# Pre-norm factors from moments gathered in the sub-layer before, and a reworked state-space stage, in a six-sub-layer decode kernel

## The chip, the cores and the metric

The kernel runs on one core of a Trainium2 chip. The number that counts is the device time of one execution in microseconds (us). The core has five engines that run beside each other, each in its own program order: TensorE (PE) multiplies matrices, VectorE (DVE), ScalarE (ACT) and GpSimd (POOL) work on elements, SyncE (SP) issues transfers. They wait for each other by semaphores.

## The reference

576 tokens (512 of a prompt, 64 of eight samples) go through six sub-layers. Each has the same frame: a root-mean-square norm ahead (pre-norm), the sub-layer, a norm behind (post-norm), and the sum with the residual.

```
def rms_norm(x, g):
    y = x * lax.rsqrt(jnp.mean(x * x, axis=-1, keepdims=True) + 1e-6)
    return y * g
# sub-layers 0, 2, 3, 5: SwiGLU, 1024 -> 2816 -> 1024
h = (silu(n @ w_gate) * (n @ w_up)) @ w_down;      x = x + 0.5 * rms_norm(h, post)
# sub-layer 1: state-space layer (S5) and a gated linear unit (GLU)
s_t = a * s_(t-1) + g * (B u_t);  y = Re(C s_t) + d * u_t          # per group of 16 channels
z = gelu(y) @ w_glu;  h = z[:1024] * sigmoid(z[1024:]);            x = x + rms_norm(h, post)
# sub-layer 4: latent attention (prompt: causal; samples: paged cache), then @ w_o
```

The data are float32. Everything that a token needs of a norm is one number: the reciprocal root of its mean square over 1024 channels.

## The kernel before

Channels lie on the partitions in eight blocks of 128, tokens along the free axis in two halves of 288. `X` is the residual, `Y` the output of the sub-layer, `XH` and `XL` (one tile, `XHL`) a high and a low part of the input of the next one. A large product is three matmuls of 288 columns (`mm3`, L156 to L158): high by high, high by low, low by high. `unit` makes 48 such matmuls (gate and up of 128 channels, one half), a down block (`down`) 33, a block of the attention's output 24. Weights come as `raw` from SP, ACT writes their high part `whi`, DVE the low part `wlo` (L151).

A norm is worked out by `stats`: the squares of all blocks are added into `ACC` (ACT squares, POOL adds, L147), a matmul with one column per 72 tokens sums over the partitions (L103; in the last block of the sub-layer its square comes as a tile of its own, `sqd`), nine small DVE operations on 72x4 elements take the reciprocal root (L107 to L116; called the chain below), a tenth writes it as a diagonal tile `rs_d` (L119), and `spread` (L127) is the matmul that lays it on all partitions, in PSUM for the post-norm, in `R` for the pre-norm.

Between two sub-layers the order is written out by hand in `tail` and `first_units` (called a boundary below). For each half: post statistics, spread, then `post` (L209 multiplies `Y` by gain and factor, L211 adds to `X`, `xsplit` writes `XH` and `XL`), then `squares` of the new `X` for the next pre-norm. Half 1's post statistics and its `post` are put off: `first_units` issues them after input blocks 0 and 2 of the next sub-layer's first four products of half 0. The gain-only input is used in the products; the pre-norm factor is multiplied in behind them, in `evac`. So a boundary has four spreads, in this order: post half 0, post half 1, pre half 0, pre half 1. There is such a boundary into sub-layers 2, 3, 4 and 5; the one into the S5 layer (sub-layer 1) is in `s5_mixer`; the last sub-layer has only its own post-norm.

The S5 layer runs as a pipeline over eight blocks k of 128 channels: `s_u` (normalized input `un`, loads), `s_a` (transpose into `TT`), `s_b` (transpose into `U`), `s_c` (product with table WV, rotation), `s_s` (scan), `s_d` (products with tables `CKb` and `mk`), `s_e` (transpose back, direct term d*u, gelu, split). Its tables are made during sub-layer 0 from a list of small pieces (`s5_pieces`); `tick`, called after each evacuation there, issues the next few, so that they lie beside the matmuls. Table parts go through DRAM: RT, CA, KT, WV; the last piece writes the table MD from KT in eight transfers (L618).

## Time and profile before

| | |
|---|---|
| time, median of 3 runs | 2487.06 us (2482.69 to 2488.77) |
| the profiled execution | 2486.95 us, its span 2485.2 us |
| TensorE busy | 2381.8 us, 96% |
| VectorE / ScalarE / GpSimd busy | 1281.5 / 873.6 / 556.1 us |
| mean granted clock of TensorE | 0.978 |

A profile is one execution. A line names the engine, the line of the kernel, the operation, the tiles (out, then in), and how many. "[1.86 <-DVE rs_d L119]" behind an instruction says that its engine sat idle 1.86 us before it, and what ended that. The granted clock is the share of full speed that TensorE got in a stretch. A matmul is pipelined: its own duration overlaps with the next, and the step from start to start is what it costs.

### The profile page before, as it was taken

What the parts mean: (1) busy time and instruction counts of PE and PEld (TensorE: products, weight loads), DVE (VectorE), ACT (ScalarE), POOL (GpSimd) and SP (SyncE); (2) the same over time, 40 slices, a digit from 0 to 9 for tenths busy, and PEclk for the clock granted to TensorE, in tenths of its full rate; (3) what the DMA queues carried; (4) which work ended last, traced back from release to release, by engine and by line L of the source; (5) the groups of instructions that cost most, each with busy time, mean ns of one, the idle gap of its engine ahead of it and who ended that gap; (6) DMA issues with size and microseconds to landing.
All of it is one profiled execution on the core that took longest, in us unless ns stands there. A gap on an engine that the chain in (4) does not pass through costs nothing.

```text
span 2485.2 us, 44160 instructions
## 1 busy us (share of the span) xinstructions
PE 2381.8 (96%) x17610; PEld 2313.1 (93%) x17610; DVE 1281.5 (52%) x2647; ACT 873.6 (35%) x1807; POOL 556.1 (22%) x819
## 2 busy tenths in 40 slices
PE   7999999789989999998999999899999999999998
PEld 7999999679989999998999999798888898999997
DVE  7564565685464233347432433767777655423434
ACT  4222322353332222224222222434666653222221
POOL 3123535452231001124100112530000042100112
PEclk9999999799989999998999999999999999999999
DMA  3224343473212222222223222345555332222221
GB/s 126 86 86 146 126 130 118 125 188 97 77 60 86 71 92 86 75 88 68 80 67 101 86 70 76 114 114 178 169 173 179 130 104 69 75 74 99 86 71 63
DMA packets 114642, 254.89 MB, mean 103 GB/s; under 512 B 25122, under 2 KB 53539, under 8 KB 114179
## 3 DMA queue, kind: packets, MB, share of 16 engines
q1 hardware_dynamic: 114434, 252.06, 32.0%
q8 instruction: 139, 2.28, 0.4%
q14 instruction: 69, 0.56, 0.1%
HBM read 231.79 MB, written 22.59 MB: 102 GB/s over the span
## 4 chain that ended last, share of the span: by engine, by line
PE 68%; DVE 6%; ACT 2%; issue 1%; POOL 1%; DMA 1%; SPq 0%; ACTq 0%; DVEq 0%; POOLq 0%
PE ps L158 20%; PE ps L156 20%; PE ps L157 20%; PE ps L1331 2%; PE ps L1296 2%; DVE XHL L153 1%; DVE t L209 1%; POOL X L211 1%; PE ps L127 1%; PE ps L1237 1%; DVE wlo L151 1%; PE ps L1317 0%; PE ps L757 0%; PE ps L1225 0%; ACT Pm L1198 0%
## 5 line engine op out<-in xcount | busy, mean ns | idle before, releaser
L156 PE MATMUL ps<-XHL,whi 128*128 128x288 f32 x3344 | 1002.4, 300 | 20.4 <-ACT whi L151 12.9
L157 PE MATMUL ps<-XHL,whi 128*128 128x288 f32 x3344 | 998.7, 299 | 4.7 <-DVE XHL L153 4.7
L158 PE MATMUL ps<-XHL,wlo 128*128 128x288 f32 x3344 | 995.9, 298 | 1.4 <-DVE wlo L151 1.4
L156 PEld LDWEIGHTS ps<-XHL,whi 128*128 128x128 f32 x3344 | 638.2, 191 | 24.3 <-ACT whi L151 13.5
L157 PEld LDWEIGHTS ps<-XHL,whi 128*128 128x128 f32 x3344 | 639.0, 191 | 9.6 <-DVE XHL L153 7.4
L158 PEld LDWEIGHTS ps<-XHL,wlo 128*128 128x128 f32 x3344 | 637.9, 191 | 2.2 <-DVE wlo L151 2.0
L151 DVE TENSOR_TENSOR wlo<-raw,whi 128x1024 fp32r<-128x1024 f32 (+2 forms) x349 | 409.3, 1198 | 317.3 <-ACT whi L151 316.6
L151 ACT ACTIVATE whi<-raw 128x1024 fp32r<-128x1024 f32 (+2 forms) x349 | 321.6, 946 | 446.0 <-PE ps L157 378.2
L158 PE MATMUL ps<-HH,wlo 128*128 128x288 f32 x1408 | 415.8, 296 | 1.9 <-DVE wlo L151 1.9
L156 PE MATMUL ps<-HH,whi 128*128 128x288 f32 x1408 | 417.3, 296 | 0.0
L157 PE MATMUL ps<-HL,whi 128*128 128x288 f32 x1408 | 415.3, 295 | 0.0
L316 POOL TENSOR_TENSOR t<-t,t 128x288 f32<-128x288 f32 x176 | 143.1, 813 | 1113.2 <-DVE t L315 983.5
L158 PEld LDWEIGHTS ps<-HH,wlo 128*128 128x128 f32 x1408 | 265.2, 188 | 2.6 <-DVE wlo L151 2.6
L156 PEld LDWEIGHTS ps<-HH,whi 128*128 128x128 f32 x1408 | 265.3, 188 | 0.4
L157 PEld LDWEIGHTS ps<-HL,whi 128*128 128x128 f32 x1408 | 265.3, 188 | 0.2
L315 DVE TENSOR_TENSOR t<-ps,R 128x288 f32<-128x288 f32 x176 | 80.2, 456 | 331.3 <-PE ps L158 331.1
L147 POOL TENSOR_TENSOR ACC<-ACC,sq 128x288 f32<-128x288 f32 x137 | 138.3, 1010 | 391.2 <-ACT sq L143 387.0
L314 ACT ACTIVATE t<-t 128x288 f32<-128x288 f32 x176 | 77.9, 444 | 329.6 <-DVE t L313 313.2
L151 ACT ACTIVATE HH<-t 128x288 fp32r<-128x288 f32 x176 | 77.2, 439 | 249.0 <-POOL t L316 242.2
L151 DVE TENSOR_TENSOR HL<-t,HH 128x288 fp32r<-128x288 f32 x176 | 81.7, 465 | 125.2 <-ACT HH L151 124.8
L313 DVE TENSOR_TENSOR t<-ps,R 128x288 f32<-128x288 f32 x176 | 79.3, 450 | 53.8 <-PE ps L158 47.9
L369 DVE TENSOR_TENSOR Y<-ps,Y 128x288 f32<-128x288 f32 x64 | 29.2, 455 | 129.4 <-PE ps L158 129.4
(332 smaller groups left out, 2612.9 us busy)
## 6 DMA issues: line engine op xcount, KB each, us to landing
raw<-GU SPq DMA_DIRECT2D x176, 512.0 KB, 4.1
pgr<-PG SPq DMA_DIRECT2D x128, 320.0 KB, 3.5
raw<-DN SPq DMA_DIRECT2D x64, 512.0 KB, 3.5
raw<-DN SPq DMA_DIRECT2D x64, 192.0 KB, 3.4
raw<-GLU SPq DMA_DIRECT2D x16, 512.0 KB, 4.2
CAd<-s5w SPq DMA_DIRECT2D x8, 576.0 KB, 3.6
WVd<-s5w SPq DMA_DIRECT2D x8, 512.0 KB, 3.4
wv<-WVd SPq DMA_DIRECT2D x8, 512.0 KB, 5.8
```

Source lines behind the costliest of these rows:

```text
L147: (add or G).tensor_tensor(acc, acc, sq, op=OP.add)
L151: return A.activation(hi, src, AF.Copy), V.tensor_tensor(lo, src, hi.bitcast(F32), op=OP.subtract)
L156: P.matmul(o, wh, xh, start=st, stop=False)
L157: P.matmul(o, wh, xl, start=False, stop=False)
L158: P.matmul(o, wl, xh, start=False, stop=sp)
L313: V.tensor_tensor(t, pp[0], R[:, hs(h)], op=OP.mult)
L314: A.activation(s, t, AF.Silu)
L315: V.tensor_tensor(u, pp[1], R[:, hs(h)], op=OP.mult)
L316: g = G.tensor_tensor(u, u, s, op=OP.mult)
L369: ins = V.tensor_tensor(y, o, y, op=OP.add)
L1296: P.matmul(so, qb[:, cb], d["kv"][u][:, :, 256 + cb * 128:384 + cb * 128], start=cb == 0, stop=False)
L1331: P.matmul(o, d["pt"][:, c], d["kv"][i // 2][:, i % 2, 0:256], start=i == 0, stop=i == 3)
```

## The change

Five things change.

1. The sum of squares of the new residual is no longer taken from the new residual. With y the post factor of a token, x' = x + y*g*Y, so the sum of x'^2 is SA + 2*y*sum(x*g*Y) + y^2*sum((g*Y)^2). `SA` (72x2x4) carries the sum of x^2 from stage to stage. During the last pass of a sub-layer `ymom` gathers, beside the sum of Y^2 in `ACC`, the other two in `R` and `ACQ`: one more ACT square, one DVE product, two more adds per block and half (POOL; the third add on DVE in the attention). `mom_a` makes the post factor and the gathered sums of a half, `mom_b` the pre factor. `squares` and the statistics ahead of a first unit go.
2. In the S5 layer half 1's `post` is done block by block inside the pipeline (`post1`), `un` is written by ACT with the gain alone, and the pre factor is multiplied in when `TT` is written, in eight ACT copies per block (two before).
3. The direct term d*u is put in the table (KO gets M16*d), so the addition in `s_e` goes; POOL's operations in the S5 loop (L730, L739, L779) go to DVE or into other operations.
4. The transfers of the table pieces (RT, CA, KT, WV and the loads of B and C) are issued some pieces behind the work that makes their data; the list has 201 pieces instead of 177 and is spread over 46 ticks instead of 52 behind the first 20.
5. `evac` of the feed-forward layers applies Silu in place.

```
+        def mom_a(h, SQ, nxt):
+
+            src = sums([[ACC[:, hs(h)], SQ[h][0]]])
+            q = cur["sm"].tile([CP, 4], F32, name="rs_a")
+            V.tensor_scalar(q, src, 1e-6, None, op0=OP.add)
+            y = rsqrt(q)
+            d = diag(y)
+            bc = None
+            if nxt is not None:
+                pbc = sums([[R[:, hs(h)], SQ[h][1]], [ACQ[:, hs(h)], SQ[h][2]]])
+                bc = cur["sm"].tile([CP, 8], F32, name="rs_bc")
+                V.tensor_copy(bc, pbc)
+            return y, d, bc
...
+        def mom_b(h, y, d_, bc):
+
+            m = cur["sm"].tile([CP, 4], F32, name="rs_m")
+            V.tensor_tensor(m, bc[:, 4:8], y, op=OP.mult)
+            V.scalar_tensor_tensor(m, bc[:, 0:4], 2.0, m, op0=OP.mult, op1=OP.add)
+            V.tensor_tensor(m, m, y, op=OP.mult)
+            V.tensor_tensor(SA[:, h], SA[:, h], m, op=OP.add)
+            V.tensor_scalar(SA[:, h], SA[:, h], 0.0, None, op0=OP.max)
+            q = cur["sm"].tile([CP, 4], F32, name="rs_ab")
+            V.tensor_scalar(q, SA[:, h], 1e-6, None, op0=OP.add)
+            return rsqrt(q, "b")
...
+        def ymom(n, m, h, y, nxt, sc=1.0):
+
+            g = GP[:, n, 1, m:m + 1]
+            out = []
+            for i, acc in enumerate((ACC, R, ACQ)):
+                dst = acc[:, hs(h)] if m == 0 else (smt("t1") if i else sqd.tile([128, H], F32, name="sqd")) if m == 7 else smt("sq")
+                if i == 1:
+                    V.scalar_tensor_tensor(dst, y, g, X[:, m, hs(h)], op0=OP.mult, op1=OP.mult)
+                else:
+                    A.activation(dst, y, AF.Square, scale=g if i else sc)
+                if 0 < m < 7:
+                    (V if n == 4 and i == 2 else G).tensor_tensor(acc[:, hs(h)], acc[:, hs(h)], dst, op=OP.add)
+                out.append(dst)
+                if nxt is None:
+                    break
+            return out
...
-            d0 = stats([ACC[:, hs(0)], SQ[0]])
+            z = [mom_a(0, SQ, nxt)]
             blk(mlast[0], 1)
...
-            squares(0, nxt, last)
-            d1 = []
-            state["pend"] = [lambda: d1.append(stats([ACC[:, hs(1)], SQ[1]])), lambda: post(n, 1, spread(d1[0]), nxt)]
+            state["mom"] = z
+            if nxt == 1:
+                s5["D0"] = mom_b(0, *z[0])
...
+                def half1():
+                    z.append(mom_a(1, SQ, nxt))
+                    spread(z[1][1], ACC[:, hs(1)])
+                    s5["D1"] = mom_b(1, *z[1])
+                    end = state["chain"].ins
+
+                    def blk1(k):
+                        with tc.issue_after(end) if k else nullcontext():
+                            post1(n, 1, ACC[:, hs(1)], nxt, k)
+                    s5["post"] = blk1
+                state["pend"] = [half1]
+                return
+            state["pend"] = [lambda: z.append(mom_a(1, SQ, nxt)), lambda: post(n, 1, spread(z[1][1]), nxt)]
...
-            d0 = stats([ACC[:, hs(0)]])
+            z = state["mom"]
+            d0 = diag(mom_b(0, *z[0]))
...
-                        d1 = stats([ACC[:, hs(1)]])
+                        d1 = diag(mom_b(1, *z[1]))
...
                 def diag():
-                    S.dma_start(s5["CA"][k], CA.rearrange("p g r d i -> p g r (d i)"))
+                    S.dma_start(s5["RT"][k], RT)
...
-                    S.dma_start(s5["KT"][k], KO)
+
+                    V.scalar_tensor_tensor(KO[:, 0:16], M16, dn[:, k:k + 1], pk[:, 0:16], op0=OP.mult, op1=OP.add)
...
+                def store():
+                    S.dma_start(s5["KT"][k], S_["KO"])
                     S.dma_start(s5["WV"][k], WT.rearrange("p g r d i -> p g r (d i)"))
-                out = [load] + [rot(i) for i in range(6)] + last
-                last[:] = [prods]
-                out += [lambda hf=hf, j=j, st=st: table(*(((CA, PW, 9, 1, hf, True), (WT, PG, 8, 0, hf, False))[st]))[j]()
+                out = [load] + [rot(i) for i in range(6)]
+                out[2:2] = last[:1]
+                out[5:5] = [bc]
+                out += last[1:2]
+                tabs = [lambda hf=hf, j=j, st=st: table(*(((CA, PW, 9, 1, hf, True), (WT, PG, 8, 0, hf, False))[st]))[j]()
                         for st in range(2) for hf in range(2) for j in range(2)]
-                return out + [diag]
+                tabs[2:2] = last[2:]
+                last[:] = [store_ca, prods, store]
+                return out + tabs + [diag]
...
-                u = UN[k] = lp.tile([128, T], F32, name="un", bufs=4)
-                if k:
-                    V.scalar_tensor_tensor(u, X[:, k], GP[:, n, 0, k:k + 1], R, op0=OP.mult, op1=OP.mult)
...
+                if k:
+                    scaled(k)
+
+            def scaled(k):
+                s5["post"](k)
+                u = UN[k] = lp.tile([128, T], F32, name="un")
+                for h in range(2):
+                    A.activation(u[:, hs(h)], X[:, k, hs(h)], AF.Copy, scale=GP[:, n, 0, k:k + 1])
...
+                u = UN.pop(k)
                 for h in range(2):
                     pt = psum()
                     for j in range(4):
-                        P.transpose(pt[:CP, (3 - j) * 128:(4 - j) * 128], UN[k][:, (4 * h + j) * CP:(4 * h + j + 1) * CP], ident)
-                    A.activation(TT[:, :, 4 - 4 * h:8 - 4 * h].rearrange("p g j i -> p j g i"),
-                                 pt[:CP].rearrange("p (j g i) -> p j g i", j=4, g=8), AF.Copy)
+                        P.transpose(pt[:CP, j * 128:j * 128 + 128], u[:, (4 * h + j) * CP:(4 * h + j + 1) * CP], ident)
+                    for j in range(4):
+                        A.activation(TT[:, :, 7 - 4 * h - j], pt[:CP, j * 128:j * 128 + 128].rearrange("p (g i) -> p g i", g=8),
+                                     AF.Copy, scale=DD[h][:, j:j + 1])
...
-                    G.tensor_tensor(m1[:, :, gq], m1[:, :, gq], m2[:, :, gq], op=OP.add)
+                    V.tensor_tensor(m1[:, :, gq], m1[:, :, gq], m2[:, :, gq], op=OP.add)
...
-                G.tensor_tensor(m1, Z, RT[:, 0:1].to_broadcast([128, 2, 4, 64]), op=OP.mult)
+                V.tensor_tensor(m1, Z, RT[:, 0:1].to_broadcast([128, 2, 4, 64]), op=OP.mult)
...
                         P.transpose(pt[:, j * CP:j * CP + CP], YT[:, 4 * h + j], ident[:CP, :CP])
-                    y, w, sq = smt("t2"), smt("t3"), smt("sq")
-                    V.scalar_tensor_tensor(y, u[:, hs(h)], s5["dn"][:, k:k + 1], pt[:, :H], op0=OP.mult, op1=OP.add)
-                    A.activation(sq, y, AF.Square)
-                    yy.append((y, w, sq))
+                    w, sq = smt("t3"), smt("sq")
+                    A.activation(sq, pt, AF.Square)
+                    yy.append((pt, w, sq))
                 for y, w, sq in yy:
-                    V.tensor_scalar(w, sq, 0.044715, 1.0, op0=OP.mult, op1=OP.add)
-                    G.tensor_tensor(w, w, y, op=OP.mult)
-                    A.activation(w, w, AF.Tanh, scale=float(np.sqrt(2 / np.pi)))
+                    V.scalar_tensor_tensor(w, sq, 1 / 0.044715, y, op0=OP.add, op1=OP.mult)
+                    A.activation(w, w, AF.Tanh, scale=float(np.sqrt(2 / np.pi) * 0.044715))
                 for h, (y, w, sq) in enumerate(yy):
-                    V.scalar_tensor_tensor(y, w, 1.0, y, op0=OP.add, op1=OP.mult)
-                    split(XH[:, k, hs(h)], XL[:, k, hs(h)], y, 0.5)
+                    V.scalar_tensor_tensor(sq, w, 1.0, y, op0=OP.add, op1=OP.mult)
+                    split(XH[:, k, hs(h)], XL[:, k, hs(h)], sq, 0.5)
...
-            end = min(len(pcs), max(done[0], 20 + (len(pcs) - 20) * (done[0] - 20) // 52))
+            end = min(len(pcs), max(done[0], 20 + (len(pcs) - 20) * (done[0] - 20) // 46))
```

The order on three engines, before and after.

On TensorE, from the S5 boundary's half-1 statistics to the first product of the S5 loop (L723 before, L785 after; `un` is the input, `TT` its transpose). Before:

```order
L127 MATMUL ps<-rs_d,ones 128x288
L103 MATMUL ps<-ones,ACC 72x1 x4
L103 MATMUL ps<-ones,sq_5476 72x1 x4
L692 MATMUL ps<-ident,un 72x128 x4
L103 MATMUL ps<-ones,sq_5478 72x1 x4
L103 MATMUL ps<-ones,sq_5480 72x1 x4
L103 MATMUL ps<-ones,sq_5482 72x1 x4
L692 MATMUL ps<-ident,un 72x128 x4
L103 MATMUL ps<-ones,sq_5484 72x1 x4
L711 MATMUL ps<-ident,TT 128x72 x8
L127 MATMUL ps<-rs_d,ones 128x288 x2
L723 MATMUL ps<-U_5559,wv 64x72 x16
```

After:

```order
L106 MATMUL ps<-ones,ACC 72x1 x4
L106 MATMUL ps<-ones,R 72x1 x4
L106 MATMUL ps<-ones,ACQ 72x1 x4
L106 MATMUL ps<-ones,sqd 72x1 x4
L106 MATMUL ps<-ones,t_5428 72x1 x4
L106 MATMUL ps<-ones,t_5430 72x1 x4
L187 MATMUL ps<-rs_d,ones 128x288
L761 MATMUL ps<-ident,un 72x128 x8
L773 MATMUL ps<-ident,TT 128x72 x8
L785 MATMUL ps<-U_5569,wv 64x72 x16
```

The six sums of the new residual's squares and two spreads between the post spread and the loop are gone; four sums stand ahead of the post spread instead.

On VectorE, at the boundary into sub-layer 3, around the diagonal tile of the pre factor of half 0. Before, from the last input splits of half 1 (`XHL`) to the first evacuation (L313):

```order
L153 SCALAR_TENSOR_TENSOR XHL<-X,GP,XHL 128x288 x4
L107 TENSOR_SCALAR rs_a<-ps 72x4
L108 TENSOR_SCALAR rs_y<-rs_a 72x4
L110 SCALAR_TENSOR_TENSOR rs_t<-rs_y 72x4
L111 TENSOR_TENSOR rs_t<-rs_t,rs_a 72x4
L112 SCALAR_TENSOR_TENSOR rs_y<-rs_t,rs_y 72x4
L113 SCALAR_TENSOR_TENSOR rs_t<-rs_y 72x4
L114 TENSOR_TENSOR rs_t<-rs_t,rs_a 72x4
L115 SCALAR_TENSOR_TENSOR rs_t<-rs_t 72x4
L116 SCALAR_TENSOR_TENSOR rs_y<-rs_t,rs_y 72x4
L119 SCALAR_TENSOR_TENSOR rs_d<-ident,rs_y 72x288
L313 TENSOR_TENSOR t_12245<-ps,R 128x288
```

After (names in `a` belong to the post factor of half 1, those in `b` to the pre factor of half 0):

```order
L121 SCALAR_TENSOR_TENSOR rs_ya<-rs_ta,rs_ya 72x4
L127 SCALAR_TENSOR_TENSOR rs_d<-ident,rs_ya 72x288
L127 SCALAR_TENSOR_TENSOR rs_d<-ident,rs_yb 72x288
L158 TENSOR_TENSOR rs_m<-rs_bc,rs_ya 72x4
L159 SCALAR_TENSOR_TENSOR rs_m<-rs_bc,rs_m 72x4
L160 TENSOR_TENSOR rs_m<-rs_m,rs_ya 72x4
L265 SCALAR_TENSOR_TENSOR t_12237<-Y,GP,ps 128x288
L265 SCALAR_TENSOR_TENSOR t_12242<-Y,GP,ps 128x288
L267 TENSOR_TENSOR X<-X,t_12237 128x288
```

The chain of the pre factor of half 0 stood behind all of half 1's post work; now its diagonal tile is written ahead of that work, beside the one of the post factor of half 1.

On GpSimd, the same boundary: adds of squares into `ACC`, adds of the post-norm into `X`, and the first gate products (L316 before, L371 after). Before:

```order
L147 TENSOR_TENSOR ACC<-ACC,sq 128x288 x7
L211 TENSOR_TENSOR X<-X,t_12081 128x288
L211 TENSOR_TENSOR X<-X,t_12086 128x288
L211 TENSOR_TENSOR X<-X,t_12091 128x288
L211 TENSOR_TENSOR X<-X,t_12101 128x288
L211 TENSOR_TENSOR X<-X,t_12106 128x288
L211 TENSOR_TENSOR X<-X,t_12111 128x288
L147 TENSOR_TENSOR ACC<-ACC,sq 128x288 x7
L316 TENSOR_TENSOR t_12247<-t_12247,t_12246 128x288
```

After:

```order
L178 TENSOR_TENSOR R<-R,sq 128x288
L178 TENSOR_TENSOR ACQ<-ACQ,sq 128x288
L267 TENSOR_TENSOR X<-X,t_12061 128x288
L267 TENSOR_TENSOR X<-X,t_12066 128x288
L267 TENSOR_TENSOR X<-X,t_12071 128x288
L267 TENSOR_TENSOR X<-X,t_12081 128x288
L267 TENSOR_TENSOR X<-X,t_12086 128x288
L267 TENSOR_TENSOR X<-X,t_12091 128x288
L267 TENSOR_TENSOR X<-X,t_12242 128x288
```

Both runs of seven adds between and behind the residual adds are gone; adds into `R` and `ACQ` stand ahead of them, in the last pass.

## Rows read from the trace of the kernel before

**Rows 1.** The page: TensorE's busy time, share of the span, instructions.

```profile
PE 2381.8 (96%) x17610; PEld 2313.1 (93%) x17610; DVE 1281.5 (52%) x2647; ACT 873.6 (35%) x1807; POOL 556.1 (22%) x819
```

**Rows 2.** TensorE's waits over the span: us in total, times, longest us.

```profile
PE ps L127 <- DVE rs_d L119: 35.2, 13, 4.8
PE ps L723 <- ACT U L712: 5.8, 5, 1.7
```

**Rows 3.** Stretches: length, TensorE busy (matmuls), granted clock, DMA share, GB/s.

```profile
1080.00:1120.00 40.00, 39.05 (x294) 1.00 0.28 90
1120.00:1160.00 40.00, 32.10 (x208) 0.83 0.16 53
```

**Rows 4.** Timeline of TensorE, boundary into sub-layer 3: start, us, instruction, idle before.

```profile
1109.89 0.65 PE L127 MATMUL ps<-rs_d,ones 72*128 72x288 f32 x2
...
1130.26 1.14 PE L127 MATMUL ps<-rs_d,ones 72*128 72x288 f32 x2 [1.86 <-DVE rs_d L119]
...
1139.28 0.40 PE L156 MATMUL ps<-XHL,whi 128*128 128x288 f32 x1 [1.65 <-ACT XHL L153]
...
1146.87 1.30 PE L127 MATMUL ps<-rs_d,ones 72*128 72x288 f32 x2 [3.70 <-DVE rs_d L119]
...
1159.38 0.65 PE L127 MATMUL ps<-rs_d,ones 72*128 72x288 f32 x2
```

**Rows 5.** Timeline of VectorE there: first and last step of two chains.

```profile
1106.69 0.16 DVE L107 TENSOR_SCALAR rs_a<-ps 72x4 f32<-72x4 f32 x1 [1.62 <-PE ps L103]
...
1108.43 0.45 DVE L119 SCALAR_TENSOR_TENSOR rs_d<-ident,rs_y 72x288 f32<-72x288 f32 x1
...
1125.62 0.14 DVE L107 TENSOR_SCALAR rs_a<-ps 72x4 f32<-72x4 f32 x1
...
1129.26 0.94 DVE L119 SCALAR_TENSOR_TENSOR rs_d<-ident,rs_y 72x288 f32<-72x288 f32 x1
```

**Rows 6.** Timeline of GpSimd there.

```profile
1124.71 7.01 POOL L147 TENSOR_TENSOR ACC<-ACC,sq 128x288 f32<-128x288 f32 x7 [2.82 <-ACT sq L143]
```

**Rows 7.** Timeline of TensorE there: a one-column sum and what follows it.

```profile
1135.33 0.62 PE L103 MATMUL ps<-ones,ACC 128*72 128x1 f32 x8
1135.81 0.38 PE L156 MATMUL ps<-XHL,whi 128*128 128x288 f32 x1
```

**Rows 8.** Timeline of TensorE, start of the S5 loop and its third and fourth step.

```profile
466.17 1.30 PE L127 MATMUL ps<-rs_d,ones 72*128 72x288 f32 x2 [4.75 <-DVE rs_d L119]
...
480.77 1.22 PE L711 MATMUL ps<-ident,TT 72*128 72x72 f32 x8 [4.14 <-ACT TT L694]
481.79 2.22 PE L127 MATMUL ps<-rs_d,ones 72*128 72x288 f32 x4
483.94 1.35 PE L723 MATMUL ps<-U,wv 128*64 128x72 f32 x18
...
503.00 1.22 PE L723 MATMUL ps<-U,wv 128*64 128x72 f32 x32
...
513.03 0.28 PE L723 MATMUL ps<-U,wv 128*64 128x72 f32 x2 [0.80 <-ACT U L712]
```

**Rows 9.** Groups of four S5 steps (503 to 543 us): busy us, mean ns, idle before.

```profile
L778 DVE TENSOR_SCALAR t<-sq 128x288 f32<-128x288 f32 x8 | 6.7, 834 | 0.2 <-ACT sq L775 0.2
L669 DVE SCALAR_TENSOR_TENSOR un<-X,GP,R 128x576 f32<-128x576 f32 x4 | 5.1, 1285 | 0.0
L740 DVE TENSOR_TENSOR Y<-Y,rt 128x512 f32<-128x512 f32 x4 | 5.1, 1277 | 0.0
L701 ACT ACTIVATE TT<-ps 72x512 f32<-72x512 f32 x8 | 4.7, 589 | 1.8 <-PE ps L700 1.8
```

**Rows 10.** The page's groups over the span: busy us, mean ns of one.

```profile
L147 POOL TENSOR_TENSOR ACC<-ACC,sq 128x288 f32<-128x288 f32 x137 | 138.3, 1010 | 391.2 <-ACT sq L143 387.0
L314 ACT ACTIVATE t<-t 128x288 f32<-128x288 f32 x176 | 77.9, 444 | 329.6 <-DVE t L313 313.2
L315 DVE TENSOR_TENSOR t<-ps,R 128x288 f32<-128x288 f32 x176 | 80.2, 456 | 331.3 <-PE ps L158 331.1
```

**Rows 11.** Timeline of VectorE, then GpSimd, in sub-layer 2's last pass.

```profile
1070.58 2.31 DVE L151 TENSOR_TENSOR wlo<-raw,whi 128x1024 fp32r<-128x1024 f32 x2 [0.55 <-ACT whi L151]
...
1071.02 1.46 POOL L147 TENSOR_TENSOR ACC<-ACC,sq 128x288 f32<-128x288 f32 x1 [3.91 <-ACT sq L143]
1075.11 0.80 POOL L147 TENSOR_TENSOR ACC<-ACC,sq 128x288 f32<-128x288 f32 x1 [2.63 <-ACT sq L143]
```

**Rows 12.** Timeline of SP's queue, end of the table work.

```profile
443.52 7.21 SPq L618 DMA_DIRECT2D MDd<-KTd  x8
```

160 lines of the change are left out of this document (70 added, 90 removed).

## The prediction, made before the changed kernel ran

> **What bounds the kernel now.** The page comes first: TensorE is busy 96% of the span [rows 1], so only two things can make the kernel faster: fewer matmuls, or less time in which TensorE is idle or slow. The change takes away few matmuls, so the next view is TensorE's waits [rows 2]. The largest by far is the spread (L127) waiting for the diagonal tile: 35.2 us in 13 waits. The third view, two neighbouring stretches of 40 us [rows 3], shows what these places cost: 294 matmuls in one, 208 in the next, which holds the boundary into sub-layer 3. At 39.05 us for 294 matmuls (0.133 each), 208 need 27.6 us. So 12.4 us are lost in that stretch: 7.9 idle (40.00 less 32.10 busy), and 4.5 because the granted clock averaged 0.83, that is, TensorE ran at 1.2 instead of 2.4 GHz for part of it. The timeline names the idle time [rows 4]: 1.86 us ahead of the post spread of half 1, 1.65 for the first input splits of half 1, 3.70 ahead of the pre spread of half 0. There are four such boundaries.
>
> The last view is VectorE there [rows 5]. The chain takes 2.19 us at 1106.69 (to the end of the diagonal tile at 1108.88) and 4.58 us at 1125.62. Beside the second run GpSimd does the seven adds of half 0's squares [rows 6]. These adds are what the change takes out.
>
> The S5 layer is the other place [rows 8]. TensorE is free at 461.42 (466.17 less 4.75), the first product of the loop starts at 483.94, and a step of the loop takes 10.03 us (503.00 to 513.03). VectorE has hardly any idle time in the loop, and two of its groups, L778 and L740, take 834 and 1277 ns [rows 9], though a VectorE operation on 288 columns takes 456 ns [rows 10].
>
> **The base.** The profiled execution took 2486.95 us, its span 2485.2. The median of the runs is 2487.06, so the sum is made from 2487.
>
> **Boundaries into sub-layers 2 to 5.** What goes: the 3.70 us wait, since the pre factor of half 0 no longer needs the new residual and its tile is written beside half 1's post tile. The 1.86 us become about 0.3, because the chain loses GpSimd's company and shrinks by 4.58 - 2.19 = 2.4 us; I leave 0.3 for the copy and the few operations of another chain that stand between. Late next are the input splits of half 1 (1.65 now), which still hang on half 1's `post`; the order now takes the products of half 1 over several banks as each split lands, and I give that 0.6 us. The 4.5 us of half speed follow the two waits that go, and I let them go too. That makes 3.7 + 1.6 + 0.6 + 4.5 = 10.4 us.
>
> What comes: six one-column sums per half instead of three. One costs 0.48 us (1135.33 to 1135.81, [rows 7]), so 3 x 0.48 x 2 = 2.9 us, all on TensorE, none hidden where it doesn't wait. The pre chain of half 1 now starts behind half 1's post work on VectorE (it was so before) and I expect a wait of 0.9 us ahead of the last spread, which had none. Net 10.4 - 2.9 - 0.9 = 6.6; four boundaries give 26 us. Ends: 2 us each if the half speed stays (8 in all), 9.5 each if the sums fall into waits and no wait comes (38).
>
> **The S5 layer's start.** Now the path is post spread, residual, squares, sums, chain, transposed copies, two pre spreads. After it is four added sums (1.9 us), spread, one block's residual, the copies of `TT`, product; the pre chain of half 1 runs on VectorE meanwhile. From 461.4: sums and chain 2.9 (the chain alone is 2.2), spread and its copy 1.7 [rows 8], a chain of some fifteen steps of 0.19 (1106.69 to 1108.43 is nine steps, [rows 5]) 2.9, residual 0.9, eight copies taking turns with transposes and products about 3, last transposes and copy 2: 474.8 us. I take 9 us of gain; ends 4 and 12.
>
> **A step of the S5 loop.** VectorE loses the normalizing product (1285 ns), two direct-term products (about 0.5 each by the 288-column row) and most of GpSimd's company; it gains a residual product and add (0.9), two adds of 256 columns (0.8) and the product of 512 columns that GpSimd did (0.7 to 1.28). From some 9.8 us (10.03 less idle time of 0.2 at most) that leaves about 8.6. ScalarE gains two copies for `un` (0.9) and eight narrow copies in place of two at 589 ns; a narrow one is not in the rows, so between 0.15 (a quarter of the wide one) and 0.44: 1.2 to 3.5 us instead of 1.2, I take 2.2. No engine then reaches 10.03, but each product waits on a round through ScalarE and VectorE, as the 0.80 us at 513.03 shows, so the step won't fall to an engine's busy time: I take 9.6, over nine steps 4 us. Ends: 1 us longer per step (9 lost) and 1.1 shorter (10 won).
>
> **The last passes.** Each block and half adds on ScalarE a square (0.44), on VectorE a product (0.46), on GpSimd two adds. A down block lasts 33 x 0.133 = 4.4 us; three adds take 2.4 us at 0.80, 4.4 us at 1.46 [rows 11]. Hidden as long as that is under the block. What is queued behind: on VectorE the evacuation of the next block and the `wlo` splits, for which TensorE waits. I price it at nothing; the other end is the slow rival below.
>
> GpSimd's add took 1.46 us beside two splits and 0.80 alone, and the splits' pair lasted 2.31 us [rows 11]. The Trainium skill, SBUF — State Buffer, section "Who interferes with whom", has a rule for this: a VectorE instruction with two inputs in SBUF and a GpSimd instruction that reads SBUF share an interface, and the one that comes second waits for the whole of the first. The trace agrees here: the splits' pair and the add together fill 1070.58 to 1072.89 as if in turn, and the add alone takes 0.80. The rule speaks against this part of the change, since the added operations are all of these kinds. In the attention's last pass, a pair of blocks is 48 x 0.133 = 6.4 us, and what would have to take turns is two products and two adds on VectorE (1.8), a split (1.2) and four adds on GpSimd (3.2): 6.2 us. That is close; for a pair of down blocks it is 0.9 + 1.8 + 4.8 = 7.5 of 8.8 us.
>
> **Table work.** It lies beside matmuls that hardly wait, before and after. On SP's queue the eight last transfers, 7.21 us of issue [rows 12], move ahead of the weight loads of two down blocks of sub-layer 0. Those loads are issued one pair of blocks ahead of need, 8.8 us, which covers 7.2 and little more; behind them waits ScalarE for `raw`, and TensorE for `whi`. Nothing, ends 4 lost and 2 won. Silu in place and the last sub-layer's tail: nothing, since neither order nor waits there change.
>
> **Sum.** 2487 - 26 - 9 - 4 = 2448 us.
>
> **Rivals.**
> (a) The half speed stays. The clock falls behind short idle times, and some remain: 0.3, about 1 for splits, 0.9 ahead of the last spread. For it: no row separates the half speed behind 3.70 us of idle from that behind 1.65. Against: the 3.70 us wait was the longest and goes. Price 4.5 x 4 = 18: 2466 us. The Trainium skill, TensorE: Matmul & The Clock Gate, "A second HAM failure mode: psum-queue depth-cycling", tells of a kernel in which short idle times between groups of matmuls were enough to keep the clock swinging; by that, this rival would hold.
> (b) The S5 loop becomes ScalarE's. Ten more activations stand in its queue, and `U`'s copy, for which TensorE already waits 5.8 us [rows 2], stands behind them. A step of 10.6 instead of 9.6: 9 us, 2457.
> (c) Slower. The last passes become GpSimd's. A block needs three adds at 1.46 and the product and square that wait for a free buffer of a ring of three, about 5.3 us; it decides from the point at which that passes 4.4. VectorE then stands in front of the splits, and TensorE waits for `wlo`. 48 down blocks x 0.9 and 16 attention blocks x 0.7 = 54 us: 2502. Against: 1.46 is met only beside splits, which are under half of the block.
> (d) It does not do what it says: the waits move on to the splits, because half 1's `post` alone sets the boundary, and the sums cost 2.9 each. Boundaries then give nothing, S5 about 5: 2482.
>
> **Chances.** Forecast 0.58 (own range 2439 to 2457), (a) 0.17, (b) 0.11, (c) 0.06, (d) 0.08. About 0.3% (7.5 us) is what a measurement of this kernel tells from no change. Faster: forecast, (a), (b) and a little of (d), 0.88; same, most of (d), 0.06; slower 0.06. The range takes in (a) and (b) and the upper ends of the boundaries: 2431 to 2473.
>
> **What would show it.** Right: TensorE's waits for the diagonal tile fall from 35 us to under 12, the pre spread of half 0 has no wait, and the 40 us stretch of a boundary holds some 250 matmuls at a clock above 0.9; the first S5 product starts near 475 and a step takes under 9.8. Wrong: a new row of waits of the input products for `XHL` or `wlo` over 10 us; a clock that stays at 0.83; GpSimd busy over nine tenths in the last passes.

## The result and the profile after

The changed kernel takes 2467.06 us (median of four runs, 2464.85 to 2468.39) against 2486.88 of the kernel before beside it: ratio 0.9922, 95% interval 0.9905 to 0.9939. It is faster by 19.8 us where 39 were forecast. The same file timed once more, in another comparison, gave 2470.66 and 0.9939 [0.9919, 0.9959], so 4 us between the medians of two kernels are not yet a difference. Executions that took far longer than the others of their kernel (8960.86 us once for this file) are left out of every median here.

The page of after, TensorE first, answers to [rows 1]; the second fence gives TensorE's waits (us in total, times, longest) and answers to [rows 2].

```profile
PE 2392.4 (97%) x17814; PEld 2326.3 (94%) x17814; DVE 1301.8 (53%) x2807; ACT 888.8 (36%) x1864; POOL 565.6 (23%) x820
```

```profile
PE ps L213 <- ACT whi L208: 16.3, 5, 8.4
PE ps L187 <- DVE rs_d L127: 10.7, 6, 2.9
PE ps L773 <- ACT TT L763: 6.6, 7, 1.9
PE ps L213 <- ACT XHL L210: 5.2, 10, 0.9
PE ps L214 <- DVE XHL L210: 4.3, 6, 1.3
...
PE ps L785 <- ACT U L774: 0.7, 1, 0.7
```

The waits for the diagonal tile fell from 35.2 to 10.7 us, those for `U` from 5.8 to 0.7. But the span shrank by 18.6 us only, and busy time on TensorE rose by 10.6: there are 204 more matmuls, and some of the time is at half clock. Two stretches of after around the boundary into sub-layer 3 (length, TensorE busy and matmuls, granted clock, DMA share, GB/s) answer to [rows 3], and the timeline of TensorE there to [rows 4]:

```profile
1066.00:1106.00 40.00, 38.67 (x302) 0.96 0.24 78
1106.00:1146.00 40.00, 37.96 (x282) 0.96 0.22 68
```

```profile
1099.32 0.65 PE L187 MATMUL ps<-rs_d,ones 72*128 72x288 f32 x2
...
1105.83 0.40 PE L214 MATMUL ps<-XHL,whi 128*128 128x288 f32 x1 [1.33 <-DVE XHL L210]
...
1107.70 0.53 PE L213 MATMUL ps<-XHL,whi 128*128 128x288 f32 x2 [0.95 <-ACT XHL L210]
...
1122.18 0.65 PE L187 MATMUL ps<-rs_d,ones 72*128 72x288 f32 x2
...
1126.13 0.65 PE L187 MATMUL ps<-rs_d,ones 72*128 72x288 f32 x2
...
1140.64 0.75 PE L187 MATMUL ps<-rs_d,ones 72*128 72x288 f32 x2
```

No spread waits here any more, the pre spread of half 0 included (3.70 us before). From the first spread to the last it is 41.32 us (49.49 before), and the second stretch holds 282 matmuls at 0.96 instead of 208 at 0.83. What is new is the 0.96 of the first stretch, which lies ahead of the boundary and had 1.00. Finer stretches of after show it: six one-column sums stand in two groups of three from 1090.1 to 1094.9, and with the second group:

```profile
1090.00:1093.00 3.00, 3.00 (x40) 1.00 0.00 0
1093.00:1097.00 4.00, 4.00 (x33) 0.68 0.02 4
1097.00:1100.00 3.00, 3.00 (x20) 0.85 0.00 0
```

TensorE is never idle in these 10 us, yet the clock is below 1.00 in the last two stretches: at its lower level, 1.2 GHz, for part of them. (The wide products start 0.24 us apart from 1094.8 to 1097.8, 0.13 on either side.)

The whole span by stages (starts of spreads and of the loop's products; forecast and measured are changes in us against before):

| stage | forecast | measured |
|---|---|---|
| start to the spread of half 0 ahead of S5 (453.64 to 465.80) | 0 | +12.2 |
| that spread to the first S5 product (30.30 to 21.36) | -9 | -8.9 |
| first to eighth step of the S5 loop (71.74 to 62.76) | -3 (-4 over nine steps) | -9.0 |
| inside the four boundaries, first spread to last | 4 x -8.05 = -32 | -9.0, -8.2, -8.4, -8.7 = -34.3 |
| ahead of the first spread of each boundary | 4 x 1.45 = +6 | +0.3, +3.9, +4.0, +12.6 = +20.8 |
| last spread of the last boundary to the end | 0 | +0.6 |

(Forecast per boundary 6.6 = 10.4 - 0.9 - 2 x 1.45; the sums of half 1 lie inside, those of half 0 ahead.) So the boundaries themselves, the S5 start and the loop came as forecast or better. 12 us were lost ahead of the S5 layer and 15 more than forecast ahead of the spreads.

### The profile page after: what moved, and what is told of

It reads as the page before. It is cut to its first block, busy times and chain, and to the rows that moved or that the text cites. A ratio compares the mean times of both kernels' runs of the same rounds, so it can differ in the third digit from the quotient of the medians.

```text
span 2466.6 us, 44725 instructions
## 1 busy us (share of the span) xinstructions
PE 2392.4 (97%) x17814; PEld 2326.3 (94%) x17814; DVE 1301.8 (53%) x2807; ACT 888.8 (36%) x1864; POOL 565.6 (23%) x820
## 5 line engine op out<-in xcount | busy, mean ns | idle before, releaser
L371 POOL TENSOR_TENSOR t<-t,t 128x288 f32<-128x288 f32 x176 | 145.0, 824 | 1086.3 <-DVE t L370 972.4
L178 POOL TENSOR_TENSOR ACC<-ACC,sq 128x288 f32<-128x288 f32 x72 | 82.4, 1144 | 314.7 <-ACT sq L176 314.7
```

The costliest lines, as they stand in the source:

```text
L178: (V if n == 4 and i == 2 else G).tensor_tensor(acc[:, hs(h)], acc[:, hs(h)], dst, op=OP.add)
L371: g = G.tensor_tensor(u, u, t, op=OP.mult)
```

## The experiments

Each kernel was timed beside the kernel before, and ratios are to it. The theory first: the missing 20 us are (i) the added one-column sums, which cost more than their length because the clock falls behind them, and the adds ahead of them in the attention's last pass; (ii) the table work's transfers, which stand on SP's queue ahead of the last weight loads of sub-layer 0. The rival to (i) is that any work added there costs its length, the rival to (ii) that ScalarE, VectorE and GpSimd are overloaded in the last pass.

**The gathered sums left out.**

```diff
-                pbc = sums([[R[:, hs(h)], SQ[h][1]], [ACQ[:, hs(h)], SQ[h][2]]])
...
-                V.tensor_copy(bc, pbc)
+                V.tensor_copy(bc[:, 0:4], src)
+                V.tensor_copy(bc[:, 4:8], bc[:, 0:4])
```

> The changed kernel without the four one-column sums of R and ACQ per half (their place in the pre factor is taken by the sum of Y squared; the adds into R and ACQ stay). It leaves out part of the computation: the pre factors are not right. This prices the sums. Theory A: a sum costs more than its 0.48 us, since TensorE falls to 1.2 GHz behind six of them (1094.8 to 1097.8 in the changed kernel, and 10 us behind the ones of the attention); then the five boundaries get 2 x 1.9 each and some 10 us of half speed: 24 to 30 us faster than the changed kernel, about 2440. Rival B: the sums cost what they last and part of it lies in waits: at most 19 us, about 2448 or more, and the half speed behind them stays.

Measured 2443.23 us, 0.983 [0.9813, 0.9846], 24 us less than after, with the adds that feed the sums still there: the lower end of theory A. From the last spread of one boundary to the first of the next it takes 391.9 us, as before (391.8; after 395.6). The sums are eight a layer, 5 x 8 x 0.5 = 20 us if all is exposed; so they cost somewhat more than their length.

**Width or length?** The four sums left out as above, and 14 unused products of 288 columns in their place:

```diff
+                dm = psum()[:, :H]
+                for g in range(14):
+                    P.matmul(dm, XH[:, g % 8, 0:128], XH[:, g % 8, hs(1)], start=g == 0, stop=g == 13)
```

> The changed kernel with the four sums of R and ACQ left out of each half and 14 unused products of 288 columns issued in their place (some 1.86 us at 0.133 each), so TensorE is busy as long as with the sums. Theory A (behind a row of one-column sums the granted clock falls, behind as much work in wide products it doesn't): clock 1.00 in the 10 us ahead of the spread into sub-layer 3 where the changed kernel has 0.68, that spread 391.93 + 1.9 = 393.8 us behind the one before it instead of 395.6, time 2455 to 2462. Theory B (any added work of that length at that place costs the same): clock near 0.7 there, 395.6 us, time 2467.

2453.42 us, 0.9874 [0.9857, 0.9892]. The clock of this kernel in the stretch ahead of the spread into sub-layer 3 (which starts at 1095.78 here):

```profile
1088.00:1092.00 4.00, 4.00 (x40) 1.00 0.02 4
1092.00:1096.00 4.00, 4.00 (x31) 1.00 0.00 0
```

It stays at 1.00, and the way from spread to spread takes 393.8 us: 1.9 more than without, the length of the products. With the sums it is 395.6, and into sub-layer 4 it is 395.7 for 393.9. So theory A holds for the boundaries into sub-layers 3 and 4: 1.9 us of length, 1.8 of clock each. The total came 2 us below A's range.

One trace of each kernel would not settle this, because the fall does not come every time. Seven of the traces here have the six sums at four places: ahead of the first spreads into the S5 layer and into sub-layers 2, 3 and 4. The clock fell at 17 of these 28 places, at a cost of 1.5 to 3.1 us each. Into sub-layer 3, from the first sum to the spread, it takes 7.7 us without a fall and 9.2 with one. In the four kernels with no added sums ahead of the spread it fell at none of 16 places, behind the wide products at none of 4. So it is the one-column sums that bring the fall, not added work of their length; whether by the one column or by their larger number of matmuls and weight loads, no run separates. After itself had the fall at two of the four places.

**The same on the kernel before.** Four unused sums, or the same 14 wide products, behind the statistics of half 0:

```diff
+            if nxt is not None:
+                dm = psum()[:CP, :16]
+                for g in range(4):
+                    for j in range(4):
+                        P.matmul(dm[:, 4 * g + j:4 * g + j + 1], ACC[:, j * CP:j * CP + CP], ones[:, 0:1], ...)
```

> The kernel before with four more one-column sums of ACC (their result is used nowhere) behind half 0's post statistics, at the end of each of the five sub-layers with a successor. They last 4 x 0.48 = 1.9 us. Theory A: a row of one-column sums makes TensorE fall to 1.2 GHz, and it stays there for some us behind it: 1.9 us and 1.5 to 2.5 more at each place, 17 to 22 us in all, 2504 to 2509; the granted clock behind the sums at about 1099 is below 0.8. Rival B: they cost what they last: 9.6 us, about 2497, clock 1.00 behind them.

> The kernel before with 14 more matmuls of 288 columns (their result is used nowhere) at the same five places; 14 x 0.132 = 1.85 us, as long as the four sums. Theory A (the sums' one column is what lets the clock fall): here the clock stays at 1.00 and the cost is 9 us, about 2496, 8 us or more below the kernel with dummy sums. Rival B (any longer stretch ahead of the spread costs the same): within 3 us of the kernel with dummy sums.

2502.25 us, 1.0081 [1.0056, 1.0107], and 2501.42, 1.0057 [1.0041, 1.0074]. By the times nothing tells sums from wide products. Stretches ahead of the boundary into sub-layer 2, of the kernel with the sums, then of that with the wide products:

```profile
668.00:672.00 4.00, 4.00 (x45) 0.91 0.01 4
672.00:676.00 4.00, 4.00 (x23) 0.66 0.00 0
```

```profile
666.00:670.00 4.00, 4.00 (x40) 1.00 0.00 0
670.00:674.00 4.00, 4.00 (x33) 1.00 0.02 4
```

Here the clock falls behind the sums alone. It does so ahead of the S5 layer too (again the sums, then the wide products):

```profile
452.00:456.00 4.00, 4.00 (x18) 0.50 0.30 91
```

```profile
452.00:456.00 4.00, 4.00 (x33) 1.00 1.06 289
```

At the other three of the five places it is 1.00 behind either. From the first sum to the spread the kernel with the sums takes 3.3 us more ahead of S5, 1.8 more ahead of sub-layer 2 and 0.2 more at the other three; the totals agree only because other stages, in which the two kernels have the same instructions, differ by as much the other way. A row of four sums is thus near an edge. Both kernels lose 15 us, more than 5 x 1.9; some 3 of it lie in the S5 loop, which the added products don't touch. That part isn't explained.

**Twice as many sums** (`range(8)` in the edit above).

> The kernel before with eight unused one-column sums behind the statistics of half 0, in five places, instead of the four of an earlier run. Theory A (a longer row of sums lowers the clock more surely): the clock falls behind the row at three or four of the four boundaries, not at one; time 2502 + 9.6 + some 3 x 3 = about 2521. Theory B (the fall at one boundary was chance): clock 1.00 at three of the four, time 2502 + 9.6 = 2512.

2527.7 us, 1.0169 [1.0151, 1.0187]. The four further sums cost 25.5 us, not their 9.6, more than either theory said: on A's side. The mean granted clock of the runs is 0.970 to 0.972; with four sums it is 0.978 or 0.979 (0.972 in one run). Where the time lies is not shown.

**Fewer and later sums.** The last block's R and ACQ are added on GpSimd too (ACQ on VectorE in the attention), so that two gathered sums per half are left, and they are issued behind the post spread (a new function):

```diff
+        def mom_c(h, z):
+            pbc = sums([[R[:, hs(h)]], [ACQ[:, hs(h)]]])
+            bc = z[2] = cur["sm"].tile([CP, 8], F32, name="rs_bc")
+            V.tensor_copy(bc, pbc)
...
-                if 0 < m < 7:
+                if 0 < m < 7 or m == 7 and i:
```

> The changed kernel with two sums of R and ACQ per half instead of four (the last block's tiles are added on GpSimd, or VectorE in the attention, like the others), issued behind the post spread of the half instead of ahead of it. Leaving all four out took 24 us from the median (2443) and 32 from the profiled span. Theory A: what costs is six sums in a row, 2.9 us in which TensorE moves one column each and behind which it falls to 1.2 GHz; apart from each other they cost what they last: five boundaries x 2 halves x 0.96 us less, and the half speed at the ends of sub-layers 2, 3 and 4 gone: 12 to 18 us less, about 2452. Rival B: any one-column sum costs the clock: then only the 9.6 us or less, 2458 or more. Rival C: two more adds at the end of each pass make R and ACQ late, TensorE waits for them in its queue: no gain.

2460.95 us, 0.99 [0.9883, 0.9916]: 6 us less than after, by the time rival B. Ahead of the spread into sub-layer 3 it is 391.9 us again, so nothing is left of the loss there; inside the boundary it is 44.0 instead of 41.3 us, and the S5 start takes 23.9 instead of 21.4, so most of it comes back later.

**The inner adds of R and ACQ left out in the attention.**

```diff
-                if 0 < m < 7:
+                if 0 < m < 7 and not (n == 4 and i):
```

> The changed kernel without the adds into R and ACQ of the inner blocks in the attention's last pass (squares and products stay; it leaves out part of the computation: the pre factors of the last sub-layer are not right). In the changed kernel this pass gains nothing: from its first product to the last pre spread 98.5 us for 98.1 before, though 6.3 us of waits for diagonal tiles are gone. Theory A: GpSimd and VectorE take turns there and run late, so the sums wait 2.2 us for ACC and R, and TensorE runs at 1.2 GHz from 2006 to 2016. Then the wait goes and most of the half speed: 6 to 9 us less, about 2459. Rival B: the half speed comes from the six sums themselves; then 2 us less, 2465.

2459.38 us, 0.9894 [0.9877, 0.9911], as theory A said. From the first product of the output projection to the first spread it takes 51.3 us before, 60.5 after, 53.3 here and 52.7 in the kernel without gathered sums. In after, TensorE waits for the adds at the sums, and the clock falls behind that:

```profile
2004.67 0.68 PE L106 MATMUL ps<-ones,ACC 128*72 128x1 f32 x8 [1.55 <-POOL ACC L178]
...
2006.00 1.12 PE L106 MATMUL ps<-ones,R 128*72 128x1 f32 x8 [0.65 <-POOL R L178]
```

```profile
2006.00:2011.00 5.00, 5.00 (x35) 0.50 0.08 33
2011.00:2016.00 5.00, 5.00 (x28) 0.50 0.00 0
```

The kernel without the inner adds has neither the wait nor the fall:

```profile
2000.00:2004.00 4.00, 4.00 (x39) 1.00 0.78 239
2004.00:2010.00 6.00, 6.00 (x65) 1.00 0.04 17
```

Why the adds are late stands in the rows of VectorE in after, the products and adds of the last pass, and in its GpSimd groups over that pass (busy, mean ns, idle before):

```profile
1993.47 1.06 DVE L174 SCALAR_TENSOR_TENSOR sq<-Y,GP,X 128x288 f32<-128x288 f32 x1
...
1995.59 1.04 DVE L174 SCALAR_TENSOR_TENSOR sq<-Y,GP,X 128x288 f32<-128x288 f32 x1 [0.69 <-POOL R L178]
```

```profile
L178 POOL TENSOR_TENSOR R<-R,sq 128x288 f32<-128x288 f32 x11 | 12.1, 1100 | 3.2 <-DVE sq L174 3.2
L178 POOL TENSOR_TENSOR ACC<-ACC,sq 128x288 f32<-128x288 f32 x11 | 11.5, 1046 | 66.8 <-ACT sq L176 66.8
```

A product takes 1.04 to 1.06 us beside an add (the group of `R<-Y,GP,X` in this pass, two that start a sum, averages 518 ns), and each then waits for a buffer that GpSimd has to free: the turn-taking by which rival (c) reckoned, for which the prediction names the Trainium skill, SBUF — State Buffer, "Who interferes with whom"; these rows agree with it. It decides in this one pass, not in the 48 down blocks.

**Table pieces one per 52 steps instead of 46** (`(done[0] - 20) // 52`), and **the Toeplitz transfers alone moved** behind the last weight loads:

```diff
-            pcs.extend([lambda: None] * 8 + last + [toeplitz])
+            pcs.extend([lambda: None] * 8 + last + [lambda: None])
+            s5["toep"] = toeplitz
...
+                if done[0] == 73 and "toep" in s5:
+                    s5["toep"]()
```

> The changed kernel with its table pieces spread over 52 ticks again instead of 46, so that the eight transfers into MD are issued behind the last weight loads of sub-layer 0. In the changed kernel the post spread of half 0 at the end of sub-layer 0 comes 12.2 us later than before (465.80 for 453.64), of which four added sums are 1.9. Theory A: SP's queue; the eight transfers (8.3 us of issue at 424.47) hold back two weight loads, ScalarE waits for raw, TensorE 2.46 + 0.77 us at 443 to 447, and then runs at 1.2 GHz to 452.6 (another 3). Then this kernel is 5 to 7 us faster than the changed one (about 2461) and the wait at 445 is gone. Rival B: the added adds and products of the last pass (ScalarE waits for the ring of squares on GpSimd) are what makes the splits late; then the spread stays at 464 to 467 and the time at 2467.

> The changed kernel with one thing moved: the eight transfers into MD stand behind the last weight loads of sub-layer 0 in SP's queue; all other table pieces keep their early places (46 ticks). With 52 ticks the wait at 445 us went, but TensorE waited 4.4 and 2.6 us for low parts at 425 and 438, since table work ran on into the last pass. Theory A: two causes, SP's queue here and VectorE's load there; with the pieces early and only the transfers late neither is met: the spread at the end of sub-layer 0 comes at 459 to 461 (465.80 in the changed kernel) and the time is 5 to 7 us less, about 2461. Rival B: the gathering alone makes sub-layer 0 late; spread at 464 or later, time within 2 us of 2467.

The first: 2473.04 us, 0.994 [0.9921, 0.9958]; TensorE's wait at 445 us is gone, but new ones for `wlo` come at 424.85 (4.41) and 437.99 (2.56), and the spread ahead of S5 starts at 469.22, later than in after. Neither theory had that. The second: 2464.88 us, 0.9907 [0.989, 0.9923], between the two theories. SP's queue, ScalarE's split and TensorE at the end of sub-layer 0 in after:

```profile
424.47 8.32 SPq L686 DMA_DIRECT2D MDd<-KTd  x8
432.89 2.33 SPq L237 DMA_DIRECT2D raw<-DN  x2
...
443.73 0.45 ACT L176 ACTIVATE sq<-Y 128x288 f32<-128x288 f32 x1 [3.52 <-DVE Y L424]
...
444.51 1.46 ACT L208 ACTIVATE whi<-raw 128x1024 fp32r<-128x1024 f32 x2
...
445.60 0.40 PE L213 MATMUL ps<-HH,whi 128*128 128x288 f32 x1 [2.46 <-ACT whi L208]
```

and SP and ScalarE in the kernel with the transfers moved:

```profile
427.88 10.21 SPq L237 DMA_DIRECT2D raw<-DN  x4
438.14 7.65 SPq L686 DMA_DIRECT2D MDd<-KTd  x8
...
434.30 1.06 ACT L208 ACTIVATE whi<-raw 128x1024 fp32r<-128x1024 f32 x1 [2.84 <-PE ps L214]
```

The weight loads are issued from 427.88 on instead of 432.89, the wait at 445 us is gone, and the spread ahead of S5 starts at 462.55 instead of 465.80. The late issue shows itself on ScalarE: in after the first of the two loads takes 7.4 us to land and is there from about 440.3 on, but the split stands behind the squares of a block that TensorE finishes at 443; with the transfers moved it stands ahead of the squares (434.30). So the trace shows a later place in ScalarE's order, and not a wait for the data alone. The spread gains only 3.3 us, because behind the six sums the clock now falls, which at this place it did not in after:

```profile
456.00:459.00 3.00, 3.00 (x17) 0.50 0.00 0
459.00:462.00 3.00, 3.00 (x14) 0.50 0.02 5
```

At the next boundary too this execution ran at half clock where the first one of after did not, and most of the gain is not in the total.

**The sums' inner part left out in sub-layer 0** (the squares, products and adds of R and ACQ of blocks 1 to 6):

```diff
+                if n == 0 and 0 < m < 7:
+                    break
```

> The changed kernel without the products, squares and adds for R and ACQ of the inner blocks in the last pass of sub-layer 0 alone (it leaves out part of the computation: the pre factors of the S5 layer are not right). Theory A: gathering is not what makes sub-layer 0 late, SP's queue is: the wait of 2.46 us at 445 stays, the spread comes at 464 to 466 and the time falls by 2 us at most. Rival B: products and adds hold up VectorE and ScalarE beside the table work: spread at 458 to 461, time 5 to 8 us less.

2463.08 us, 0.9901 [0.9873, 0.993]; its runs lie 14 us apart, so the time doesn't tell. The wait for `whi` stays (2.03 us), and the spread starts at 464.75, 1 us earlier; two kernels with the same sub-layer 0 as after start it at 464.80 and 465.69. So the engines' added work isn't what makes sub-layer 0 late: theory A.

**The S5 loop.** The partial sum and the 512-column product given back to GpSimd in the changed kernel; and the kernel before with both on VectorE and its two operations for the polynomial of the gelu folded into one. Of the first edit:

```diff
...
-  V.tensor_tensor(m1, Z, RT[:, 0:1].to_broadcast([128, 2, 4, 64]), op=OP.mult)
+  G.tensor_tensor(m1, Z, RT[:, 0:1].to_broadcast([128, 2, 4, 64]), op=OP.mult)
```

> The changed kernel with two operations of the S5 loop back on GpSimd: the add of m1 and m2 and the product of Z and RT (the other parts of the S5 change stay). The step of the loop fell from 10.0 to 9.3 us, from first to last product 71.7 to 62.8 us. Theory A: the step was VectorE's, slowed by GpSimd's company; then the step goes back to 9.7 to 10.2 us and the time up by 3 to 7 us. Rival B: the step is set by the round through ScalarE and TensorE, and the shorter gelu and the direct term in the table made it shorter; then step and time stay within 1 us.

> The kernel before with one part of the change alone: in the S5 loop the add of m1 and m2 and the product of Z and RT are on VectorE, and GpSimd's product in the gelu is folded into one VectorE operation. A step took 10.03 us, with VectorE busy nearly all of it. Theory A: GpSimd's company costs VectorE more than the work that it takes over; the step falls to 9.3 to 9.7 us and the time by 3 to 6 us (about 2482). Rival B: VectorE is the bound by its own work, and gets 1.6 us more of it: the step rises to 10.5 or more, the time by 3 us or more.

With GpSimd back: 2472.76 us, 0.9942 [0.9924, 0.996], first to eighth step in 66.9 us (after 62.8, before 71.7), the last four steps 10.0 to 10.2 us each: theory A. Before without GpSimd: 2478.33 us, 0.9965 [0.9951, 0.9979], its first to eighth step 8.6 us shorter: theory A, and more than it said. Four steps of before, of after, and of before without GpSimd (length; busy time of TensorE, its weight loads, VectorE, ScalarE, GpSimd; clock, DMA):

```profile
503.00:543.10 40.10, 34.09 (x353) 27.87 (x352) 37.06 (x65) 21.64 (x61) 23.11 (x27) 1.00 0.81 212
```

```profile
503.39:540.65 37.26, 34.42 (x353) 27.85 (x352) 29.68 (x68) 29.63 (x94) 3.79 (x9) 1.00 0.70 194
```

```profile
503.00:538.60 35.60, 33.99 (x353) 27.89 (x352) 33.39 (x77) 22.99 (x63) 5.15 (x7) 1.00 0.84 230
```

VectorE is busy for 37.1 of 40.1 us before; taking work from GpSimd onto VectorE makes VectorE's busy time shorter (33.4 us for 77 operations instead of 65), and a step falls to 8.9 us, near the 8.5 that TensorE is busy. Nearly all that the loop gains can be had by this edit alone; its steps are even shorter than those of after (8.9 us for 9.3).

**Both remedies together, then with the spacing too.**

> The changed kernel with two late sums per half (as in e8_two_late_sums, 2461) and the MD transfers behind the last weight loads (as in e7_md_last, 2465). Theory A: the two remedies meet different places (end of sub-layer 0; five boundaries) and add up: 3 us more than the late sums alone, 2456 to 2459, lower than both kernels. Rival B: what is won at the end of sub-layer 0 is lost again behind the GLU, where TensorE ran at 1.2 GHz for some 7 us in e7 and e8 and not in the changed kernel: 2460 to 2464.

> The version with both remedies (Toeplitz transfers behind the last weight loads; two gathered sums per half behind the post spread) and the table pieces issued one per 52 steps instead of 46. Theory A (what is still late at the end of sub-layer 0, 1.8 us against the kernel before, is the spacing of table work): the first spread comes near 454 and the time falls to 2453 to 2455. Theory B (the spacing was a matter of the Toeplitz transfers alone; later pieces run into the last pass): the first spread at 455 to 460, time 2456 to 2462.

Two late sums with the Toeplitz transfers moved: 2456.6 us, 0.9891 [0.9872, 0.9909], the fastest kernel that computes everything, 10.5 us below after: theory A. The spread ahead of S5 starts at 455.42 (453.64 before), with no wait in the last pass. With 52 steps per piece it is 2460.66, 0.9905 [0.9888, 0.9923]: waits for `wlo` of 4.39 and 1.36 us come back, and the spread starts at 461.15. So the closer spacing wasn't at fault.

**The changed kernel again.**

> The changed kernel itself once more. In its first profile the boundary into sub-layer 2 takes 41.6 us from the first spread to the fourth, at full clock; in e7 and e8 and three others 45 to 46, with TensorE at 1.2 GHz for part of it, though no instruction of that boundary differs in most of them. Theory A: the place stands at the edge of a fall of the clock, and the same kernel shows either: 41.6 or 46.1 here, with runs spread over 4 us or more. Rival B: what differs ahead of it in the kernel decides: 41.6 again, and runs within 2465 to 2469.

2470.66 us, as said, with runs from 2467.43 to 2474.4. The boundary into sub-layer 2, in this execution, then in that of after:

```profile
670.00:675.00 5.00, 3.21 (x21) 0.88 0.00 2
675.00:680.00 5.00, 5.00 (x30) 0.50 0.15 25
```

```profile
670.00:675.00 5.00, 2.65 (x19) 1.00 0.05 19
675.00:680.00 5.00, 5.00 (x53) 1.00 0.03 7
```

The same instructions, at 1.2 GHz in one and at 2.4 in the other (44.7 and 41.6 us for the boundary): theory A. The other boundaries agree within 0.2 us between the two.

## Why the prediction was wrong, step by step

The mechanisms were mostly right, the size was not: -19.8 us for -39. The stated range, 2431 to 2473, holds the time only because it takes in rival (a).

**Boundaries, inside: right.** The waits for the diagonal tile go as forecast (3.70 to 0, 1.86 to 0; at the last spread none into sub-layer 3 and 1.33 into sub-layer 4, for 0.9). Those for the input splits stay: into sub-layer 3 TensorE waits 3.1 us in all for `XHL`, 3.3 before, where 1 us was to go. In sum 34.3 us came for 32.

**The sums: mis-sized, the first step that failed.** "One costs 0.48 us ... so 3 x 0.48 x 2 = 2.9 us" took a row of sums for its length. The count is right for a whole boundary (four come ahead of each post spread, the one of the pre-norm goes), but the four all stand ahead of the spread, and into sub-layers 3 and 4 another 1.8 us of half clock follow the 1.9 of their length. "The 4.5 us of half speed follow the two waits that go, and I let them go too" is true of the place and false of the sum: the half clock moved ahead of the first spread. Rival (a) named the effect but hung it on idle time; here TensorE was never idle. That its 2466 us lie next to the measured 2467 is luck: the half speed that it kept inside the boundaries mostly went, and the loss lies elsewhere.

**The last passes: "I price it at nothing" failed in one of them.** In the attention's, for which 6.2 of 6.4 us had been worked out, the adds come late, TensorE waits 1.55 and 0.65 us at the sums, and 10 us at half clock follow: 9.1 us. Taking away the sums or the adds gives back 7 to 8 of it. With the wide products in place of the sums the clock falls there as well (0.55 from 1995 to 2000), behind a wait of 1.39 us; in the three kernels with late sums, which have no added sums ahead of this spread, it falls behind a wait of 1.72 to 1.81 (0.50 from 2002 to 2006 with the late sums alone). With neither sums nor wide products a wait of 1.19 us leaves it at 1.00. So here the fall goes with the wait for the adds, with or without the sums; what the sums add to it is not shown. A further 3.5 us of the 12.6 lie earlier in the attention, from the last spread of the boundary into it to the output projection (377.2 us, 373.8 before). The sums don't explain them: the changed kernel has them in both of its traces, but four kernels with the same attention and the same sums take 374.1 to 375.7. Their cause stays open.

**Table work: "Nothing, ends 4 lost and 2 won" failed.** The row for it was there [rows 12]: 7.21 us of issue against a cover of 8.8. They became 8.32 us, the last loads were issued 5 us later than they could be, and the spread ahead of S5 came 12.2 us late. Of these, 10.0 lie ahead of the first sum (458.16 for 448.15). With the transfers moved it comes at 451.84; kernels that leave sub-layer 0 as in after reach it at 455.64 to 458.16, so the transfers are worth 3.8 to 6.3 us. The waits at 445 us are 2.5 + 0.8 us; around and behind them the granted clock is 0.80 (440 to 450) and 0.86 (450 to 460). The other 2.1 us, from the first sum to the spread (7.6 for 5.5), are the four added sums of half 0, for which the forecast had no term at this boundary. With the transfers moved this way takes 10.7, by the fall of the clock; with the late sums it is 5.5 again. So both remedies together take away 10.4, and each alone less (3.3 and 5.0). What is left of the 10.0 us is not settled.

**S5's start: right** (-8.9 for -9; without the 12.2 us it would be 475.0 against 474.8 forecast). The row of the loop's start in after, which answers to [rows 8]:

```profile
479.82 1.32 PE L187 MATMUL ps<-rs_d,ones 72*128 72x288 f32 x2 [2.04 <-DVE rs_d L127]
...
487.16 2.19 PE L785 MATMUL ps<-U,wv 128*64 128x72 f32 x32
...
503.39 1.22 PE L785 MATMUL ps<-U,wv 128*64 128x72 f32 x32
...
512.66 1.22 PE L785 MATMUL ps<-U,wv 128*64 128x72 f32 x32
```

**S5's step: under-sized.** 9.27 us (503.39 to 512.66) for 9.6 forecast, and over the eight steps -9.0. VectorE needs 7.4 us a step instead of the 8.6 reckoned, since its operations are shorter without GpSimd beside them (1277 ns for a 512-column product [rows 9], 683 in after). The forecast read 9.8 us of work and at most 0.2 idle in a step of before; the stretch above shows 9.3 and 0.8 (37.06 of 40.10 in four steps). With the other terms as it had them (- 1.3 - 1.0 + 0.9 + 0.8 + 0.7) this leaves 9.4, so by an estimate from these numbers GpSimd's company was worth 2 us a step, where the forecast's 8.6 gave it 0.8. Rival (b)'s 10.6 did not come: a narrow copy takes 372 ns, towards the upper bound, but ScalarE is busy for 29.6 of 37.3 us only. It has a point all the same: TensorE's only wait in these four steps is for those copies (`TT`), 2.8 us in all. The two groups in four steps of after:

```profile
L801 DVE TENSOR_TENSOR Y<-ACQ,rt 128x512 f32<-128x512 f32 x4 | 2.7, 683 | 0.0
...
L763 ACT ACTIVATE TT<-ps,rs_yb 72x128 f32<-72x128 f32 x32 | 10.4, 372 | 0.0
```

## What to carry to other kernels

Price a row of very narrow matmuls by what follows it, not by its own length: look at the granted clock in stretches of 3 to 5 us behind each. When transfers are moved on a queue, count what stands behind them against its due time; here 8.8 us of cover over 7.2 us of issue was not enough. Where two engines take turns, try giving the work to one: here it was faster with all of it.

## What the runs showed of the hardware

The clock fell from 2.4 to 1.2 GHz while TensorE was busy without a gap, behind six one-column sums (0.68 over 4 us), and not behind products of 288 columns for as long (1.00). It is an edge: behind the six it fell at 17 of 28 places, behind four more in the kernel before at two of five, and at one boundary the same instructions ran at 1.00 in one execution and at 0.50 in another. GpSimd beside VectorE cost the S5 loop more time than the work that it took off: 37.06 us of VectorE for 65 operations with it, 33.39 for 77 without.
